# Layer 1's gate and up projections as seven block products instead of eight, in a one-core inference step

## The chip, the core and the metric

One core of a Trainium2 chip runs the kernel. The metric is the device time of one execution in microseconds, as the median of three runs. Engines are named as the profile names them: PE (TensorE), DVE (VectorE), ACT (ScalarE), POOL (GpSimd) and SP (SyncE, which issues most of the DMAs).

## What is computed

The reference is one inference step of a two-layer backbone: 512 latent tokens and 128 context tokens of width 1024 pass, in each of two layers, through four token mixers and then a gated feed-forward part. The change lies in the feed-forward part of the second layer (layer 1, counted from 0):

```python
def modulated_norm(x, g, shift, scale):
    return rms_norm(x, g) * (1 + scale) + shift

def ffn_sublayer(x, mods, p):
    h = modulated_norm(x, p['norm2_g'], mods[3], mods[4])
    y = (jax.nn.silu(h @ p['ffn_w_gate']) * (h @ p['ffn_w_up'])) @ p['ffn_w_down']
    return x + mods[5] * y
```

The widths are 1024 for the model and 2816 for the inner part. Everything is float32.

## The kernel before, in words

All 640 tokens are handled together, with features on the 128 partitions and tokens along the free dimension. A float32 matrix product is made of three matmuls in the type float32r: each operand is kept as a high part `hi` (the value cast) and a low part `lo` (the value less `hi`), and hi·hi, hi·lo and lo·hi are added in PSUM. `split` (L307) makes the two parts: the cast on ACT (L308), the subtraction on DVE (L309). `weights` (L311) brings one 128-column piece of a weight matrix (128 x 8 x 128, 512 KB) into one of three `wst` buffers by a DMA on SP and splits it into one of two `whi` and `wlo` buffers; `spare` (L325) names other tiles for the last down-projection pieces.

The feed-forward part of a layer (in `run`, from L2090) has 22 inner tiles f of 128 columns. For each, `fm_tile` (L619) makes the gate product and then the up product: 8 slices of the width times 3 matmuls times 2 token halves (256 and 384 columns), 48 matmuls each, so 96 for a tile. ACT takes silu of the gate product (L2120), DVE multiplies it with the up product out of PSUM (L2128), and the result `g` is split. The tiles run in three parts (8, 7, 7). After each part, the down projection adds the part's product to the residual `x` (L1810), in 8 output tiles e.

The first tile is special: `by_halves` (L648) makes the gate and up products of tile 0 and the gate product of tile 1 over the first 256 tokens, and during that time the norm of the other 384 tokens is finished: their sum of squares by matmul (`nst`), a reciprocal square root in eleven small DVE instructions (L377 to L383), a broadcast by matmul (`nb`), and then `norm_k` (L564) for each of the 8 slices: scaling on DVE (L571), the `hi` part on ACT (L574), and the `lo` part on DVE for even slices (L580) or, over a shifted copy made by ACT (L578), on POOL for odd ones (L584). POOL also adds the squares (L541).

PE's order of work is written out in the program. On the other engines the tile framework's scheduler sets the order; each engine then runs its queue strictly in that order, and an instruction that waits holds up what is behind it. `g`, `sg` and `h` are SBUF tiles; `acc` and `tacc` are PSUM tiles (five banks in turn for the projections).

## Time and profile before

| | |
|---|---|
| median of three runs | 1959.8 us (1953.36 to 1960.69) |
| the profiled execution | 1962.85 us, of which the span of instructions is 1961.0 us |
| PE busy / DVE / ACT / POOL over the span | 94% / 55% / 37% / 17% |
| granted PE clock, mean over the span | 0.978 |

The profile gives, for each engine, busy time, what its instructions wait for, and the chain of waits that ended last, followed back from the last instruction. A matmul row of a timeline merges neighbours of one shape: the time from one row's start to the next is what PE spent, while the duration shown includes the pipeline behind the last one. Durations of DVE and ACT instructions overlap by some hundredths of a microsecond with the next one's.

### The profile page before, as it was taken

To read this page: it belongs to the slowest core of one execution; us is meant where nothing else is said; L and a number is where in the kernel's file an instruction comes from. 1 tells how busy PE (TensorE), PEld (TensorE's weight loads), DVE (VectorE), ACT (ScalarE), POOL (GpSimd) and SP (SyncE) were. 2 spreads that over 40 slices of the span, in tenths; PEclk is the share of its full clock that TensorE was granted. 3 is DMA by queue.
4 is the path that set the end of the run, shared out by engine and by line. 5 is a ranking of instruction groups with operands and counts; after the bars stand their busy time and mean duration, and the time that the engine had idled before them with its cause. 6 is when DMAs were issued, how large, how long until landed. Compare 5 with 4: busy or idle time off the path is not lost.

```text
span 1961.0 us, 40272 instructions
## 1 busy us (share of the span) xinstructions
PE 1847.3 (94%) x16620; PEld 1742.0 (89%) x16620; DVE 1070.1 (55%) x2304; ACT 727.5 (37%) x1497; POOL 329.7 (17%) x530
## 2 busy tenths in 40 slices
PE   5998998899999999999999999789999999999997
PEld 4986787778999999999998988678889999999997
DVE  6573546677557547647555854567655232233244
ACT  4632124766442112222346322367645221221231
POOL 1221521233300000000133271123322000000001
PEclk9997899999999999999999999899999999999999
DMA  7345423142445436436423322213342222222221
GB/s 299 122 119 135 125 78 104 31 110 79 139 138 172 140 108 193 150 109 189 133 91 101 98 66 67 77 44 84 95 151 65 76 76 76 76 68 83 75 97 54
DMA packets 114166, 210.35 MB, mean 107 GB/s; under 512 B 44160, under 2 KB 61312, under 8 KB 113856
## 3 DMA queue, kind: packets, MB, share of 16 engines
q1 hardware_dynamic: 105920, 202.74, 32.8%
q0 software_dynamic: 2816, 4.72, 1.2%
q8 instruction: 130, 2.13, 0.4%
q10 hardware_dynamic: 5248, 0.33, 0.2%
q14 instruction: 52, 0.43, 0.1%
HBM read 183.14 MB, written 19.89 MB: 104 GB/s over the span
## 4 chain that ended last, share of the span: by engine, by line
PE 78%; DVE 9%; ACT 5%; DMA 5%; issue 2%; POOL 1%; SPq 0%; DVEq 0%; ACTq 0%; POOLq 0%
PE acc L351 56%; PE tacc L351 6%; PE pvo L351 2%; PE ptp L363 2%; PE sc L351 2%; PE mpart L351 1%; PE invp L351 1%; DMA wst<-wout 1%; DVE wlo L309 1%; ACT p L1294 1%; ACT whi L308 1%; DMA wmd<-wmodT 1%; DMA wmd<-wmod 1%; ACT pt L1329 1%; PE ysp L351 1%
## 5 line engine op out<-in xcount | busy, mean ns | idle before, releaser
L351 PE MATMUL acc<-h,whi 128*128 128x256 f32 (+1 forms) x3520 | 679.0, 312 | 3.2 <-ACT h L574 1.4
L351 PEld LDWEIGHTS acc<-h,whi 128*128 128x128 f32 x3520 | 578.5, 189 | 11.7 <-issue 3.4
L308 ACT CAST whi<-wst 128x1024 fp32r<-128x1024 f32 (+3 forms) x202 | 196.9, 976 | 687.9 <-PE acc L351 645.0
L351 PE MATMUL acc<-h,wlo 128*128 128x256 f32 (+1 forms) x1760 | 411.1, 310 | 0.8 <-DVE wlo L309 0.8
L309 DVE TENSOR_TENSOR wlo<-wst,whi 128x1024 fp32r<-128x1024 f32 (+3 forms) x202 | 229.9, 1139 | 204.2 <-ACT whi L308 199.3
L351 PEld LDWEIGHTS acc<-h,wlo 128*128 128x128 f32 x1760 | 320.4, 189 | 2.5 <-DVE wlo L309 1.3
L351 PE MATMUL acc<-g,whi 128*128 128x256 f32 (+1 forms) x1128 | 216.7, 309 | 0.1
L541 POOL TENSOR_TENSOR sq<-sq 128x256 f32<-128x256 f32 (+1 forms) x48 | 45.4, 947 | 927.2 <-ACT sq L535 926.9
L1810 DVE SCALAR_TENSOR_TENSOR x<-acc,mods,x 128x256 f32<-128x256 f32 (+1 forms) x192 | 75.3, 434 | 210.6 <-PE acc L351 210.4
L351 PEld LDWEIGHTS acc<-g,whi 128*128 128x128 f32 x1128 | 185.9, 188 | 0.4 <-DVE g L309 0.4
L507 DVE SCALAR_TENSOR_TENSOR wmj<-wmd,cb 128x1024 f32<-128x1024 f32 x112 | 136.8, 1222 | 40.9 <-DMA wmd<-wmodT 39.6
L351 PE MATMUL tacc<-whi,h 128*128 128x256 f32 (+1 forms) x640 | 151.2, 317 | 1.0 <-ACT whi L308 0.8
L351 PE MATMUL acc<-g,wlo 128*128 128x384 f32 (+1 forms) x564 | 135.2, 309 | 0.0
L351 PEld LDWEIGHTS tacc<-whi,h 128*128 128x128 f32 x640 | 111.4, 194 | 11.8 <-issue 6.6
L351 PE MATMUL acc<-oh,whi 128*128 128x384 f32 (+1 forms) x512 | 114.6, 314 | 3.3 <-DVE xe L1810 1.9
L363 PE MATMUL ptp<-cbase,p 128*128 128x128 f32 x512 | 80.3, 283 | 27.8 <-ACT pt L1329 14.1
L351 PEld LDWEIGHTS acc<-g,wlo 128*128 128x128 f32 x564 | 103.2, 188 | 0.0
L351 PE MATMUL tacc<-wlo,h 128*128 128x256 f32 (+1 forms) x320 | 98.2, 307 | 1.3 <-DVE wlo L309 1.3
L363 PEld LDWEIGHTS ptp<-cbase,p 128*128 128x128 f32 x512 | 56.6, 141 | 43.9 <-ACT pt L1329 17.6
L2128 DVE TENSOR_TENSOR sg<-acc,sg 128x256 f32<-128x256 f32 x88 | 39.2, 485 | 101.9 <-PE acc L351 101.9
L1297 POOL TENSOR_SCALAR dg<-cbase,sd 128x128 f32<-128x128 f32 x96 | 58.8, 613 | 207.1 <-DVE sd L1295 150.0
L1294 ACT ACTIVATE p<-sc,sm 128x768 f32<-128x768 f32 (+1 forms) x96 | 79.8, 831 | 31.8 <-DVE sm L1291 23.6
(321 smaller groups left out, 2655.9 us busy)
## 6 DMA issues: line engine op xcount, KB each, us to landing
wmd<-wmodT SPq DMA_DIRECT2D x56, 512.0 KB
wst<-wg SPq DMA_DIRECT2D x44, 512.0 KB
wst<-wu SPq DMA_DIRECT2D x44, 512.0 KB
wmd<-wmod SPq DMA_DIRECT2D x40, 512.0 KB
wst<-wd SPq DMA_DIRECT2D x34, 448.0 KB
wst<-wfm SPq DMA_DIRECT2D x24, 512.0 KB
wst<-wd SPq DMA_DIRECT2D x16, 512.0 KB
wst<-wtma SPq DMA_DIRECT2D x12, 512.0 KB
```

The lines of the kernel that those rows point to most:

```text
L308: self.nc.scalar.copy(hi, src)
L309: self.nc.vector.tensor_tensor(out=lo, in0=src, in1=hi.bitcast(F32), op=ALU.subtract)
L351: self.nc.tensor.matmul(out, lhsT, rhs, start=start, stop=stop)
L363: self.nc.tensor.transpose(out, in_, self.ident)
L507: nc.vector.scalar_tensor_tensor(out=j, in0=st, scalar=1.0, in1=self.cb[:, g], op0=ALU.mult, op1=ALU.mult, accum_out=self.msum[:, e, g:g + 1])
L541: (eng or nc.gpsimd).tensor_tensor(out=self.sq[hf][0], in0=self.sq[hf][0], in1=sq, op=ALU.add)
L1294: nc.scalar.activation(p, s, AF.Exp, bias=m, accum_out=d)
L1297: nc.gpsimd.tensor_scalar(out=dg, in0=self.ident, scalar1=d, scalar2=None, op0=ALU.mult)
L1329: nc.scalar.copy(pt[:, a:a + m].rearrange("p a b -> p (a b)"), tp[:, :128 * m])
L1810: self.nc.vector.scalar_tensor_tensor(out=x_out[:, a:b], in0=o[h][:, a - HB * h:b - HB * h], scalar=m[:, 8 * gate + e, grp:grp + 1], in1=x ...
L2128: nc.vector.tensor_tensor(out=sg[:, s], in0=ou[q], in1=sg[:, s], op=ALU.mult)
```

## The change

In layer 1, tiles 3 to 21 are made by a scheme of Strassen's kind. Stack the gate and up pieces of a tile as two block rows, cut the width into two halves of four slices and the tokens into two halves of 320 columns. The 2 x 2 block product, which takes eight block products (each 4 slices x 3 matmuls), is made from seven, of sums of blocks.

- Tokens, once: the norm of the last 384 tokens leaves its float32 result in new tiles `hraw` (`raw`, made by ACT for all slices), POOL adds `hi` and `lo` of the first 256 tokens to have their float32 values too (`raw_tokens`, four instructions of 512 columns), and during tile 0 DVE forms four sums in two steps (`sums_of_tokens`, eight instructions of 640 columns), of which three are split into the new tile `tt`. The fourth replaces half of `h` after tile 2 (`last_sum`).
- Weights, for each tile (`seven`): four sums on POOL (L771 to L774 of the changed kernel), and seven splits of 512 columns, five by ACT and DVE and two by ACT and POOL. The split operands go in turn through six pairs' worth of `whi`, `wlo` and `sw` buffers. The raw pieces have a fourth buffer (`wsx`).
- Results: one copy from PSUM on ACT and seven DVE additions from PSUM of 320 columns (L798 to L810) put the four blocks together; silu then works in SBUF, and the product with the gate is taken in SBUF (L2236).
- There are 8 instead of 12 `g` tiles in layer 1, and the last down-projection pieces find their room in `sw` and `tt` (`room`); the first two of them are split after tile 21 in the program's text, before it until now.

The core of the diff:

```diff
+    def room(self, e, l, pool, n):
+        if e == 0:
+            ts = [pool.tile([128, KD, 128], F32R, tag="sw", name="w2", bufs=2) for _ in range(2)]
+        elif e == 2:
+            t = self.left_room = pool.tile([128, 3, 2, 4, HT], F32R, tag="tt", name="w2", bufs=1)
+        if 2 <= e < 6:
...
-    def norm_k(self, l, which, hf, k, x, rb, h, pool):
+    def norm_k(self, l, which, hf, k, x, rb, h, pool, raw=None):
...
-            if k % 2:
+            if raw:
+                nc.scalar.activation(raw[:, a:b], t[:, a:b], AF.Identity, bias=bias)
+            elif k % 2:
...
             else:
...
-        if k % 2:
+        if k % 2 or raw:
             s = SPLIT[hf]
-            nc.gpsimd.tensor_tensor(out=lo[:, s], in0=t[:, s], in1=hi[:, s].bitcast(F32), op=ALU.subtract)
+            eng = nc.gpsimd if k % 2 else nc.vector
+            eng.tensor_tensor(out=lo[:, s], in0=(raw or t)[:, s], in1=hi[:, s].bitcast(F32), op=ALU.subtract)
...
+    def raw_tokens(self, h, pool):
+        self.raw = [pool.tile([128, 2, T], F32, tag="g", name="hraw", bufs=self.gbufs) for _ in range(4)]
+        for p in range(4):
+            v = [h[:, q, 2 * p:2 * p + 2, 0:HB] for q in range(2)]
+            self.nc.gpsimd.tensor_tensor(out=self.raw[p][:, :, 0:HB], in0=v[0].bitcast(F32), in1=v[1].bitcast(F32),
+                                         op=ALU.add)
+    def sums_of_tokens(self, h, pool):
...
+        tt = pool.tile([128, 3, 2, 4, HT], F32R, tag="tt", name="tt", bufs=1)
+        v = self.nc.vector.tensor_tensor
+        for p in range(2):
+            b11, b12 = self.raw[p][:, :, left], self.raw[p][:, :, right]
+            b21, b22 = self.raw[p + 2][:, :, left], self.raw[p + 2][:, :, right]
+            v(out=b11, in0=b12, in1=b11, op=ALU.subtract)
+            v(out=b12, in0=b22, in1=b12, op=ALU.subtract)
+            v(out=b22, in0=b22, in1=b11, op=ALU.subtract)
+            v(out=b21, in0=b21, in1=b22, op=ALU.subtract)
+            for i, t in enumerate((b22, b12, b21)):
+                self.split(*[tt[:, i, q, 2 * p:2 * p + 2] for q in range(2)], t)
...
+    def last_sum(self, h):
+        for p in range(2):
+            self.split(*[h[:, q, 2 * p:2 * p + 2, HT:T] for q in range(2)], self.raw[p][:, :, 0:HT])
+    def seven(self, srcs, acc, pool):
...
+        nc = self.nc
+        raw = []
+        for src in srcs:
+            self.raws += 1
+            r = (pool.tile([128, KD, 128], F32, tag="wsx", name="wst", bufs=1) if self.raws % 4 == 3 else
+                 self.wp.tile([128, KD, 128], F32, tag="wst", name="wst", bufs=3))
+            nc.sync.dma_start(out=r, in_=src)
+            raw += [r[:, 0:4], r[:, 4:8]]
+        a11, a12, a21, a22 = raw
+        def slot():
+            i = self.slots = (self.slots + 1) % 3
+            p, tag = ((self.wp, "whi"), (self.wp, "wlo"), (pool, "sw"))[i]
+            t = p.tile([128, KD, 128], F32R, tag=tag, name="sw", bufs=2)
+            return t[:, 0:4], t[:, 4:8]
...
+        g, v = nc.gpsimd.tensor_tensor, nc.vector.tensor_tensor
+        w = {}
+        w["a11"], w["s2"], w["a12"], w["s3"], w["s1"], w["a22"] = [slot() for _ in range(6)]
+        def by_pool(hi, lo, src):
+            nc.scalar.copy(hi, src)
+            g(out=lo, in0=src, in1=hi.bitcast(F32), op=ALU.subtract)
+        s2, s3, s4 = [pool.tile([128, 4, 128], F32, tag=t, name="sum", bufs=1) for t in ("s2", "s3", "s4")]
+        g(out=s3, in0=a11, in1=a21, op=ALU.subtract)
+        g(out=a21, in0=a21, in1=a22, op=ALU.add)
+        g(out=s2, in0=a21, in1=a11, op=ALU.subtract)
+        g(out=s4, in0=a12, in1=s2, op=ALU.subtract)
+        self.split(*w["a11"], a11)
+        self.split(*w["s2"], s2)
+        by_pool(*w["a12"], a12)
+        self.split(*w["s3"], s3)
+        self.split(*w["s1"], a21)
+        by_pool(*w["a22"], a22)
+        def product(a, b):
+            o = acc.tile([128, 512], F32, tag="w", name="acc")[:, 0:HT]
+            wt, tok = w[a], self.tokens[b]
+            for k in range(4):
+                for c, (i, j) in enumerate(((0, 0), (0, 1), (1, 0))):
+                    self.mm(o, wt[i][:, k], tok[j][:, k], k == 0 and c == 0, k == 3 and c == 2)
+            return o
+        sg = pool.tile([128, T], F32, tag="sg", name="sg", bufs=3)
+        up = pool.tile([128, T], F32, tag="sg", name="up", bufs=3)
+        c11, c12, c21, c22 = sg[:, 0:HT], sg[:, HT:], up[:, 0:HT], up[:, HT:]
...
+        p1 = product("a11", "b11")
+        w["s4"] = slot()
+        self.split(*w["s4"], s4)
+        p6 = product("s2", "t2")
+        nc.scalar.copy(c11, p1)
+        v(out=c12, in0=p6, in1=c11, op=ALU.add)
+        p2 = product("a12", "b21")
+        v(out=c11, in0=p2, in1=c11, op=ALU.add)
+        nc.scalar.activation(c11, c11, AF.Silu)
+        p7 = product("s3", "t3")
...
+        p5 = product("s1", "t1")
+        v(out=c22, in0=p5, in1=c21, op=ALU.add)
+        v(out=c12, in0=p5, in1=c12, op=ALU.add)
+        p4 = product("a22", "t4")
...
+        p3 = product("s4", "b22")
+        v(out=c12, in0=p3, in1=c12, op=ALU.add)
+        nc.scalar.activation(c12, c12, AF.Silu)
+        return sg, up
...
             gpool, g_st = self.pool("g", side="left")
+            by_sums = l == L - 1
+            plain = 3 if by_sums else KF
+            self.gbufs = 8 if by_sums else 12
...
                 last = lambda e, n=f1 - f0: self.weights(A["wd"][l, e, :, f0:f1], [128, n, 128],
-                                                         parts=self.spare(e, l, gpool, n))
+                                                         parts=(self.room if by_sums else self.spare)(e, l, gpool, n))
                 for f in range(f0, f1):
+                    if f >= plain:
+                        if f == plain:
+                            self.last_sum(h)
+                        sg, up = self.seven([A["wg"][l, f], A["wu"][l, f]], ps, gpool)
+                        g[f - f0] = gt = gpool.tile([128, 2, T], F32R, tag="g", name="g", bufs=self.gbufs)
+                        if f < KF - 1:
+                            nc.vector.tensor_tensor(out=up, in0=up, in1=sg, op=ALU.mult)
+                            self.split(gt[:, 0], gt[:, 1], up)
+                            continue
+                        for s in (slice(0, HT), slice(HT, T)):
+                            nc.vector.tensor_tensor(out=up[:, s], in0=up[:, s], in1=sg[:, s], op=ALU.mult)
+                            self.split(gt[:, 0, s], gt[:, 1, s], up[:, s])
...
@@ -2108,21 +2253,25 @@
                         def second():
                             rb = self.bcast(1, r[0], ps)
                             for k in range(KD):
-                                self.norm_k(l, 1, 1, k, x, rb, h, fx)
-
+                                self.norm_k(l, 1, 1, k, x, rb, h, fx, by_sums and self.raw[k // 2][:, k % 2])
+                        if by_sums:
+                            self.raw_tokens(h, gpool)
...
                         self.modulate(f, gpool)
-                    g[f - f0] = gt = gpool.tile([128, 2, T], F32R, tag="g", name="g", bufs=12)
+                    if by_sums and f == 0:
+                        self.sums_of_tokens(h, gpool)
+                    g[f - f0] = gt = gpool.tile([128, 2, T], F32R, tag="g", name="g", bufs=self.gbufs)
...
                 for e in range(2, KD):
                     done(e, e, halves[0], self.plain(steps(e, halves[0])))
-                kept.pop(2)
-                for i, e in enumerate((6, 7, 0, 1, 3, 4, 5, 2)):
+                again = 1 if by_sums else 2
+                kept.pop(again)
+                for i, e in enumerate((6, 7, 0, 3 - again, 3, 4, 5, again)):
```

The order of instructions shows the move at three places. The first is PE in the middle of the feed-forward part. Before, one product of a tile alternates between its two token halves, in rows of one matmul; `acc` is the bank, `whi` and `wlo` the split weight, `h` the tokens (the 48 rows of the product go on in this way):

```order
L351 MATMUL acc_19239<-h_16966,whi_19235 128x256
L351 MATMUL acc_19240<-h_16966,whi_19235 128x384
L351 MATMUL acc_19239<-h_16966,whi_19235 128x256
L351 MATMUL acc_19240<-h_16966,whi_19235 128x384
L351 MATMUL acc_19239<-h_16966,wlo_19236 128x256
```

Now, a whole tile (each `sw` is one pair of split operands, `tt` the token sums):

```order
L366 MATMUL acc_18069<-h_16966,sw_18042 128x320 x12
L366 MATMUL acc_18085<-tt_17685,sw_18043 128x320 x12
L366 MATMUL acc_18100<-h_16966,sw_18044 128x320 x12
L366 MATMUL acc_18115<-tt_17685,sw_18045 128x320 x12
L366 MATMUL acc_18129<-h_16966,sw_18046 128x320 x12
L366 MATMUL acc_18144<-tt_17685,sw_18047 128x320 x12
L366 MATMUL acc_18158<-h_16966,sw_18082 128x320 x12
```

In place of 96 matmuls of 256 and 384 columns in turn stand 84 of 320, in seven runs of twelve, each with a bank and an operand pair of its own.

The second place is DVE for one tile in the middle of the feed-forward part. Before (L2128 is the product with silu out of PSUM, L309 a split's subtraction, `g` the result):

```order
L2128 TENSOR_TENSOR sg_19230<-acc_19239,sg_19230 128x256
L2128 TENSOR_TENSOR sg_19230<-acc_19240,sg_19230 128x384
L309 TENSOR_TENSOR wlo_19356<-wst_19353,whi_19355 128x1024
L309 TENSOR_TENSOR g_19289<-sg_19230,g_19289 128x640
L309 TENSOR_TENSOR wlo_19417<-wst_19414,whi_19416 128x1024
```

Now (L310 is the split's subtraction, `sum` a weight sum made by POOL, L798 to L810 the additions out of PSUM):

```order
L310 TENSOR_TENSOR sw_19349<-sum_19354,sw_19349 128x512
L803 TENSOR_TENSOR up_19235<-acc_19282,sg_19234 128x320
L805 TENSOR_TENSOR up_19235<-acc_19296,up_19235 128x320
L806 TENSOR_TENSOR sg_19234<-acc_19296,sg_19234 128x320
L310 TENSOR_TENSOR sw_19351<-sum_19355,sw_19351 128x512
L808 TENSOR_TENSOR up_19235<-acc_19311,up_19235 128x320
L310 TENSOR_TENSOR sw_19352<-wst_19346,sw_19352 128x512
L810 TENSOR_TENSOR sg_19234<-acc_19325,sg_19234 128x320
L2236 TENSOR_TENSOR up_19235<-up_19235,sg_19234 128x640
L310 TENSOR_TENSOR sw_19388<-sum_19356,sw_19388 128x512
L310 TENSOR_TENSOR g_19340<-up_19235,g_19340 128x640
```

Five instructions a tile have become fourteen (the next tile's first two additions and two splits, interleaved in the same way, complete them), and the weight splits of the next tile stand between this tile's additions.

The third place is DVE in tile 0, from the last norm instruction (`nt`) to the split of the up piece of tile 1 (`wlo` out of `wst`). Before:

```order
L571 SCALAR_TENSOR_TENSOR nt_17563<-nb_17507,oms1_77,x_16970 128x128
L580 SCALAR_TENSOR_TENSOR h_16966<-nt_17556,mods1_75,h_16966 128x256
L580 SCALAR_TENSOR_TENSOR h_16966<-nt_17556,mods1_75,h_16966 128x128
L309 TENSOR_TENSOR wlo_17684<-wst_17681,whi_17683 128x1024
```

Now (two of the eight subtractions, L725, stand ahead of these rows):

```order
L726 TENSOR_TENSOR hraw_17420<-hraw_17422,hraw_17420 128x2x320
L727 TENSOR_TENSOR hraw_17422<-hraw_17422,hraw_17420 128x2x320
L602 TENSOR_TENSOR h_16966<-hraw_17423,h_16966 128x384
L728 TENSOR_TENSOR hraw_17422<-hraw_17422 128x2x320
L726 TENSOR_TENSOR hraw_17421<-hraw_17423,hraw_17421 128x2x320
L310 TENSOR_TENSOR tt_17685<-hraw_17420,tt_17685 128x640
L727 TENSOR_TENSOR hraw_17423<-hraw_17423,hraw_17421 128x2x320
L310 TENSOR_TENSOR tt_17685<-hraw_17422,tt_17685 128x640 x2
L310 TENSOR_TENSOR tt_17685<-hraw_17421,tt_17685 128x640
L728 TENSOR_TENSOR hraw_17423<-hraw_17423 128x2x320
L310 TENSOR_TENSOR wlo_17717<-wst_17714,whi_17716 128x1024
```

The weight's split now stands behind eight subtractions of token sums and four of the six splits of them.

## Rows read from the trace of the kernel before

**Rows 1.** The page: busy time and instructions of each engine; the chain's shares by engine.

```profile
PE 1847.3 (94%) x16620; PEld 1742.0 (89%) x16620; DVE 1070.1 (55%) x2304; ACT 727.5 (37%) x1497; POOL 329.7 (17%) x530
...
PE 78%; DVE 9%; ACT 5%; DMA 5%; issue 2%; POOL 1%; SPq 0%; DVEq 0%; ACTq 0%; POOLq 0%
```

**Rows 2.** Two stretches of layer 1's feed-forward part (columns in the first row).

```profile
core 0: us, PE busy (x) PEld busy (x) DVE busy (x) ACT busy (x) POOL busy (x), PEclk, DMA share, GB/s
1525.00:1595.00 70.00, 70.00 (x482) 70.00 (x481) 20.38 (x25) 17.45 (x26) 0.00 (x0) 1.00 0.25 76
1798.60:1896.60 98.00, 98.00 (x674) 98.00 (x673) 32.66 (x40) 27.80 (x39) 0.00 (x0) 1.00 0.27 91
```

**Rows 3.** SP's waits, 1500 to 1961: line <- awaited: total us, times, longest.

```profile
SPq L315 <- DVE wlo L309: 375.4, 58, 20.7
...
SPq L315 <- DMA wst<-wg: 3.1, 1, 3.1
```

**Rows 4.** DVE's timeline, two tiles in succession: start, duration, instruction, [wait <- awaited].

```profile
1553.06 0.89 DVE L2128 TENSOR_TENSOR sg<-acc,sg 128x256 f32<-128x256 f32 x2 [4.84 <-PE acc L351]
...
1567.06 0.89 DVE L2128 TENSOR_TENSOR sg<-acc,sg 128x256 f32<-128x256 f32 x2 [4.84 <-PE acc L351]
```

**Rows 5.** PE's timeline in an earlier stage with matmuls of 432 columns.

```profile
1056.38 0.56 PE L351 MATMUL tacc<-whi,h 128*128 128x432 f32 x2
...
1056.98 0.55 PE L351 MATMUL tacc<-whi,h 128*128 128x432 f32 x2
```

**Rows 6.** POOL: one line's group (shortest/mean/longest ns), two instructions of the timeline.

```profile
L966 POOL TENSOR_TENSOR decay<-cbase,fg x10: 1038/1365/2020, 94.6 to 1077.6; 128x512 f32<-128x512 f32 x10
...
1479.34 0.73 POOL L584 TENSOR_TENSOR h<-nt,h 128x256 fp32r<-128x256 f32 x1
...
1490.88 1.02 POOL L584 TENSOR_TENSOR h<-nt,h 128x384 fp32r<-128x384 f32 x1 [10.81 <-ACT nt L578]
```

**Rows 7.** DVE's groups by form: ... xcount | busy us, mean ns | idle ahead.

```profile
L309 DVE TENSOR_TENSOR g<-sg,g 128x640 fp32r<-128x640 f32 x42 | 34.4, 819 | 0.0
...
L2128 DVE TENSOR_TENSOR sg<-acc,sg 128x384 f32<-128x384 f32 x44 | 24.1, 548 | 0.0
...
L2128 DVE TENSOR_TENSOR sg<-acc,sg 128x256 f32<-128x256 f32 x44 | 18.6, 423 | 101.9 <-PE acc L351 101.9
...
L309 DVE TENSOR_TENSOR wlo<-wst,whi 128x512 fp32r<-128x512 f32 x26 | 17.8, 696 | 10.8 <-ACT whi L308 10.8
```

**Rows 8.** ACT's groups by form.

```profile
L308 ACT CAST g<-sg 128x640 fp32r<-128x640 f32 x42 | 30.7, 731 | 43.8 <-DVE sg L2128 42.6
...
L2120 ACT ACTIVATE sg<-acc 128x384 f32<-128x384 f32 x44 | 21.3, 484 | 0.0
...
L308 ACT CAST whi<-wst 128x512 fp32r<-128x512 f32 x26 | 15.8, 615 | 19.0 <-DMA wst<-wout 11.4 <-PE acc L351 6.6 <-DVE oh L348 1.1
```

**Rows 9.** Timeline: DVE and POOL at work at once, two places.

```profile
1465.54 1.00 POOL L541 TENSOR_TENSOR sq<-sq 128x384 f32<-128x384 f32 x1 [4.53 <-ACT sq L535]
...
1465.67 0.88 DVE L383 SCALAR_TENSOR_TENSOR nr<-rsa,nr 128x2 f32<-128x2 f32 x1
...
1477.28 1.23 DVE L309 TENSOR_TENSOR wlo<-wst,whi 128x1024 fp32r<-128x1024 f32 x1
...
1478.21 1.16 POOL L541 TENSOR_TENSOR sq<-sq 128x384 f32<-128x384 f32 x1 [1.88 <-ACT sq L535]
```

**Rows 10.** Timeline of tile 0: the second half's norm.

```profile
1482.10 1.22 DVE L309 TENSOR_TENSOR w<-wst,w 128x1024 fp32r<-128x1024 f32 x1
...
1485.69 0.16 DVE L383 SCALAR_TENSOR_TENSOR nr<-rsa,nr 128x3 f32<-128x3 f32 x1
...
1486.44 0.83 PE L351 MATMUL nb<-cbase,nr 128*128 128x128 f32 x6
```

**Rows 11.** Timeline: the split of tile 1's up piece, and PE behind it.

```profile
1503.16 1.23 DVE L309 TENSOR_TENSOR wlo<-wst,whi 128x1024 fp32r<-128x1024 f32 x1 [6.70 <-ACT whi L308]
...
1504.44 0.56 PE L351 MATMUL acc<-h,wlo 128*128 128x256 f32 x2 [0.41 <-DVE wlo L309]
```

More of the change, by code (lines that the diff above doesn't have):

```diff
@@ L27 @@
 SPLIT = (slice(0, HB), slice(HB, T))
+HT = T // 2
 L = 2
@@ L338, in spare @@
         return [t[:, 0:128 * n].rearrange("p (k n) -> p k n", k=n) for t in ts]
+    def room(self, e, l, pool, n):
[4 more added lines that the diff above has]
+        if 2 <= e < 6:
+            t = self.left_room.rearrange("p a b c d -> p (a b c d)")
+            ts = [t[:, 128 * n * i:128 * n * (i + 1)] for i in (2 * e - 4, 2 * e - 3)]
+        elif e:
+            return None
+        ts = [t.rearrange("p a b -> p (a b)") if len(t.shape) == 3 else t for t in ts]
+        return [t[:, 0:128 * n].rearrange("p (k n) -> p k n", k=n) for t in ts]
     def put(self, oh, k, a, src, view=None):
@@ L685, in half_steps @@
         return o
+    def raw_tokens(self, h, pool):
[5 more added lines that the diff above has]
+    def sums_of_tokens(self, h, pool):
+        left, right = slice(0, HT), slice(HT, T)
+        tt = pool.tile([128, 3, 2, 4, HT], F32R, tag="tt", name="tt", bufs=1)
[9 more added lines that the diff above has]
+                self.split(*[tt[:, i, q, 2 * p:2 * p + 2] for q in range(2)], t)
+        b = lambda q, k, s: h[:, q, 4 * k:4 * k + 4, s]
+        self.tokens = {
+            "b11": [b(q, 0, left) for q in range(2)], "t1": [b(q, 0, right) for q in range(2)],
+            "b21": [b(q, 1, left) for q in range(2)], "b22": [b(q, 1, right) for q in range(2)],
+        }
+        for i, n in enumerate(("t2", "t3", "t4")):
+            self.tokens[n] = [tt[:, i, q] for q in range(2)]
@@ L2093, in run @@
             gpool, g_st = self.pool("g", side="left")
+            by_sums = l == L - 1
+            plain = 3 if by_sums else KF
+            self.gbufs = 8 if by_sums else 12
+            self.slots = self.raws = -1
             for part, (f0, f1) in enumerate(THIRDS):
@@ L2102, in run @@
                         r = []
-                        parts = [gpool.tile([128, 2, T], F32R, tag="g", name="w2", bufs=12).rearrange("p a t -> p (a t)")
+                        parts = [gpool.tile([128, 2, T], F32R, tag="g", name="w2", bufs=self.gbufs).rearrange("p a t -> p (a t)")
                                  [:, 0:D].rearrange("p (k n) -> p k n", k=KD) for _ in range(2)]
@@ L2117, in run @@
                         og = self.fm_tile(A["wg"][l, f], lambda q, k: h[:, q, k], range(KD), ps)
-                    sg = gpool.tile([128, D], F32, tag="sg", name="sg", bufs=3)[:, :T]
+                    sg = gpool.tile([128, T if by_sums else D], F32, tag="sg", name="sg", bufs=3)[:, :T]
                     for q in range(2):
```

4 lines of the change are left out of this document (added).

## The prediction, made before the changed kernel was run

> **What bounds the kernel now.** I began with the page. PE is busy 94% of the span and holds 78% of the chain of waits, while DVE has little more than half its time filled and POOL a sixth [rows 1]. Such averages cover many stages, so I looked at the stage that changes. In two stretches of layer 1's feed-forward part PE is busy for all of the time at a granted clock of 1.00 (2.4 GHz); DVE works 29 to 33% of it, ACT 25 to 28%, POOL not at all, and the DMA share is about a quarter [rows 2]. The transfers are not near a limit: SP's waits are nearly all for buffers to be split (375.4 us over 58 waits, behind DVE), and the one transfer that is waited for itself costs 3.1 us [rows 3]. So here a shorter stream of matmuls is a shorter kernel, as long as POOL, DVE and ACT can feed it.
>
> **What a matmul costs.** The same pair of DVE instructions comes at 1553.06 and at 1567.06 [rows 4]: a tile takes 14.00 us, and with 96 matmuls, half of 256 and half of 384 columns, that is 0.1458 us for a mean of 320 columns. Whether 320 columns are priced by columns could be doubted, since no such matmul is in this trace. An earlier stage has 432: its pattern of three repeats after 0.60 us (1056.38 to 1056.98) [rows 5], so 0.200 each, 0.463 ns a column. The tiles give 0.1458/320 = 0.456 ns. Two widths agree within 2%, so I take price by columns.
>
> **The change part by part.**
>
> *PE.* A tile goes from 96 to 84 matmuls of 320 columns on the average: 84 x 0.1458 = 12.25 us, 1.75 less. Nineteen tiles (3 to 21) give **-33.25 us**. The bounds: at the rate of the 432 columns 84 x 320 x 0.463 ns = 12.45, so -29.5; 33.25 is the other end.
>
> *What must fit in 12.25 us.* POOL makes six instructions of 512 columns a tile. It has two rows of the same kind at 256 and 384 columns, 0.73 and 1.02 us; the line through them gives 1.31 at 512. The only rows of 512, on another line, go from 1.038 to 2.020 with a mean of 1.365 [rows 6]. I take 1.31, nearest in kind and close to that mean: 7.86 us a tile. DVE: five splits of 0.696, seven additions out of PSUM that lie between 0.423 (256) and 0.548 (384), so 0.486, and the product and the split of `g` at 0.819 each [rows 7]: 3.48 + 3.40 + 1.64 = 8.52. ACT: seven casts of 0.615, three instructions of 320 columns at 0.484 or less, one cast of 0.731 [rows 8]: 4.31 + 1.45 + 0.73 = 6.49. Each alone fits, POOL with 4.4 us to spare.
>
> *Chains between them.* A pair of split operands is filled again for the product six places on, so from the end of one use to the next stand five products, 5 x 1.75 = 8.75 us. Refilling takes a cast and a subtraction, 0.615 + 0.696 on DVE or + 1.31 on POOL, behind whatever else those queues hold; about 5 us are over. So I cost it at nothing; the cover is PE's five products, and were it gone, a product would start late by what the queues add. The raw weights land some 3 us after issue and are asked for a tile ahead. At the switches of the parts (after tiles 7, 14 and 21) the down projection needs the last tile's `g` only after six or seven of its slices, so I cost these at nothing as well, and the two weight pieces that are split after tile 21 instead of before at 0 to 1 us.
>
> *The port that DVE and POOL share.* POOL is new in this stage. Where the two already meet, a POOL instruction of 384 columns that starts at 1478.21 beside a DVE split that ends at 1478.51 takes 1.16 instead of 1.02 us; so 0.14 of the 0.30 us that they shared were lost and 0.16 were gained. A small DVE instruction that starts inside a POOL one takes 0.88 instead of 0.16 and ends as POOL ends [rows 9, 10]. The rows, then, show a wait for most of the other's duration. By them I count the instructions of both engines that read SBUF with two inputs as lying end to end, less 0.16 for each: POOL's six (7.86), DVE's five splits (3.48), its product and `g` split (1.64), 12.98 in all; less 13 x 0.16 = 2.08, makes 10.90, under 12.25. DVE's additions out of PSUM are not among them (one input is PSUM), and no row here has one beside POOL. If they held the port too, 3.40 more would make 14.3 us, more than the old tile; this is part of the slower rival below.
>
> The Trainium skill (SBUF — State Buffer, "Who interferes with whom") says that a DVE instruction with two SBUF inputs and a GpSimd instruction that reads SBUF exclude each other fully, for the whole instruction. By that rule the 0.16 falls away and the tile takes 12.98 us. The row with 1.16 speaks for a little less than that.
>
> *The start, tile 0.* It gets new work in two places where PE already waits on a chain. (a) POOL's four additions of 512 columns (4 x 1.31 = 5.24 us) start as soon as the first half is normed, about 1480, and meet the DVE split at 1482.10 and then the eleven small instructions that end at 1485.69 + 0.16. PE takes their result at 1486.44, so 0.59 us are spare [rows 10]. By turns of add, split, add, split, add and then the small ones between the rest, the last ends about 1488.7: 2.85 later, **+2.3** for PE. Bounds: 0, if POOL goes first and the splits slip into the gaps, and 5.24 - 0.59 = 4.6, if all four go ahead. (b) The split of tile 1's up piece, which PE waits 0.41 us for, comes on DVE after 6.70 us of idle time [rows 11]. Now eight subtractions and four splits of 640 columns stand ahead: 12 x 0.819 = 9.83; 9.83 - 6.70 = **+3.1**. Bounds: 0 (the norm's subtractions on the same queue become fewer, and idle time elsewhere takes some), and 4.8 with all six splits ahead. The norm's extra ACT instructions lie beside DVE's work in both bounds.
>
> *The sum:* -33.25 + 2.3 + 3.1 = **-27.85 us**. The profiled execution took 1962.85 us (span 1961.0), so 1935.0 for one like it. The median of the runs shown lies 3.05 below that execution, so I forecast **1932.0**. The bounds of the start alone (0 to 9.4) and of the column price (up to 3.8 less gained) give 1926.5 to 1939.8.
>
> **The rivals.**
>
> 1. *The port is held for whole durations.* The tile takes 12.98; 1.02 x 19 = 19.4 gained, 5.4 lost: -14.0, so 1945.8. For it: the small instruction that waited for all of POOL's [rows 9]. Against it: the 0.16 beside, and gaps in which only additions out of PSUM are due. It is what the page of the Trainium skill named above states. Chance 0.17.
>
> 2. *POOL becomes the bound (slower).* If POOL's 512 columns stretch beside a busy DVE, which they share the port with, the tile's period is POOL's six durations plus some 4.0 us in which DVE's and POOL's turns cannot overlap: the 5.12 of DVE's seven two-input instructions less 7 x 0.16. It equals the old 14.00, less 5.4/19 for the start, at (13.72 - 4.0)/6 = 1.62 us an instruction; above that the kernel is slower. At the slowest row of that width, 2.02 [rows 6], it is 16.1: 2.1 x 19 + 5.4 = +45, so 2005. The same place is reached if additions out of PSUM hold the port (14.3: +0.3 x 19 + 5.4 = +11, 1971). For it: the spread of those ten rows. Against: their mean, 1.365, and the rows of POOL in the norm. Chance 0.08.
>
> 3. *320 columns cost as much as 384.* From rows 4, 384 columns cost 0.175: a tile 84 x 0.175 = 14.7, +0.7 x 19 + 5.4 = +19, so 1978. Against: the 432 columns [rows 5]. Chance 0.03.
>
> 4. *In-order queues eat the gain.* Each engine has one queue, and an addition that waits for a product holds up the next tile's splits behind it. If each tile lost 1.5 us so, 0.25 x 19 - 5.4 would be left, so no change. Against: 5 us of slack for each operand. Chance 0.07.
>
> 5. *The start is hidden:* -33.25, so 1926.5. Chance 0.05.
>
> **How the numbers follow.** The forecast has the remaining 0.60. The range runs from 1924 (case 5, and some of the spread of the runs) to 1950 (case 1 with the start at its upper bound of 9.4): it leaves out cases 2 to 4, 0.18. A measurement of this kernel can tell about 0.5% from no change, 9.8 us: faster is below 1950.0, slower above 1969.6. The forecast, 1 and 5 are faster (0.82); 4 is the same (0.07); 2 and 3 are slower (0.11).
>
> **What would show it.** Right: in a stretch of tiles 8 to 20, the first addition from PSUM recurs every 12.25 us, PE is busy all the time at clock 1.00, POOL is at 60 to 65%, DVE near 70%. Rival 1 shows as a period near 13 with PE waiting for a split operand, on DVE and POOL in turn; rival 2 as POOL without idle time, instructions of 512 columns above 1.6 us, and PE waiting for line 768's results or those behind lines 773 and 774; rival 3 as PE at 100% with a period of 14.7. The start shows as two waits of PE, about 2.3 us ahead of the broadcast and 3.5 ahead of tile 1's up product. I am wrong altogether if PE's clock falls in the stretch, because waits in each tile break up its stream.

## The result and the profile after

| | before | changed |
|---|---|---|
| median of four runs | 1960.24 us | 1937.92 us (1936.36 to 1942.35) |
| the profiled execution, span | 1962.85, 1961.0 us | 1942.35, 1940.6 us |

The ratio is 0.9894, with a 95% interval of 0.9862 to 0.9926: 22.3 us less by the medians. A second set of runs gave 0.9872 (0.983 to 0.9915). The time lies in the forecast's range (1924 to 1950), 5.9 us above the forecast of 1932.0.

The page of the changed kernel, engines and chain, as in [rows 1]:

```profile
PE 1820.8 (94%) x16392; PEld 1714.9 (88%) x16392; DVE 1219.8 (63%) x2488; ACT 784.7 (40%) x1627; POOL 512.7 (26%) x648
...
PE 77%; DVE 9%; ACT 5%; DMA 5%; issue 2%; SPq 0%; POOL 0%; DVEq 0%; ACTq 0%; POOLq 0%
```

PE is 26.5 us shorter in busy time, DVE 149.7 and POOL 183.0 longer, and neither of the two holds more of the chain. By stretches (columns as in [rows 2]), five tiles of the second part and the 4.4 us behind a wait of tile 1:

```profile
1666.70:1728.20 61.50, 61.50 (x423) 61.50 (x421) 55.10 (x71) 30.40 (x55) 45.57 (x29) 1.00 0.26 79
1514.32:1518.70 4.38, 4.38 (x19) 4.38 (x20) 3.75 (x5) 1.35 (x2) 0.21 (x1) 0.61 0.63 180
```

PE has no idle time in the tiles, at a granted clock of 1.00. But DVE shows 90% and POOL 74% of the stretch. Their instructions have grown longer, as the groups by form of the changed kernel show (xcount | busy us, mean ns):

```profile
L310 DVE TENSOR_TENSOR sw<-sum,sw 128x512 fp32r<-128x512 f32 x57 | 56.8, 996 | 6.7 <-ACT sw L309 6.7
L310 DVE TENSOR_TENSOR sw<-wst,sw 128x512 fp32r<-128x512 f32 x38 | 46.5, 1223 | 8.7 <-ACT sw L309 8.2
...
L310 DVE TENSOR_TENSOR g<-up,g 128x640 fp32r<-128x640 f32 x18 | 26.8, 1488 | 2.2 <-ACT g L309 2.2
...
L805 DVE TENSOR_TENSOR up<-acc,up 128x320 f32<-128x320 f32 x19 | 9.3, 492 | 4.8 <-PE acc L366 2.9 <-DVE up L803 0.5
...
L803 DVE TENSOR_TENSOR up<-acc,sg 128x320 f32<-128x320 f32 x19 | 9.1, 480 | 3.1 <-PE acc L366 3.1
...
L768 POOL TENSOR_TENSOR sw<-wst,sw 128x512 fp32r<-128x512 f32 x38 | 57.2, 1504 | 94.0 <-ACT sw L767 52.9 <-PE acc L366 41.1
L773 POOL TENSOR_TENSOR sum<-wst 128x512 f32<-128x512 f32 x19 | 32.5, 1712 | 0.4
```

A split of 512 columns takes 0.996 to 1.223 us beside POOL and 0.696 without it, one of 640 columns 1.488 and 0.819 [rows 7]; POOL's 1.5 to 1.7 compare with some 1.3. DVE's additions with one input in PSUM take 0.48 to 0.49, which is what the 0.423 and 0.548 of [rows 7] for 256 and 384 columns give for 320. So a busy share in this profile contains the time for which an instruction waits for the other engine.

**Where the time went.** The rest of this document measures the stage, from PE's first matmul on `h` in layer 1's feed-forward part to the end. In the two executions of the changed kernel that were profiled it took 456.47 us both times; every other kernel's stage is known from one execution. What runs before it are the same instructions in all kernels here, yet they ended between 1474.84 and 1489.79 us; differences of whole times of a few us say nothing about the stage. PE's rows at the second part's ends:

```profile
1654.40 1.92 PE L366 MATMUL acc<-h,sw 128*128 128x320 f32 x12
1656.16 1.92 PE L366 MATMUL acc<-tt,sw 128*128 128x320 f32 x12
...
1740.50 0.75 PE L366 MATMUL acc<-g,whi 128*128 128x256 f32 x4
```

| piece of the stage, us | before | changed |
|---|---|---|
| first matmul on `h` to tile 3 | 45.12 | 52.29 |
| tiles 3 to 7 | 70.00 | 61.69 |
| tiles 8 to 14 | 98.00 | 86.10 |
| tiles 15 to 21 | 97.99 | 86.38 |
| two down projections, and all behind tile 21 | 170.01 | 170.01 |
| stage | 481.12 | 456.47 |

(Before, tile 3 has no mark of its own; its start is the first down projection's less five tiles of 14.00, and the matmul after three tiles of 96 starts at that time.) So the tiles gave 31.8 us, the start took 7.2 back, and the remaining pieces are the same. The start lost its time here:

```profile
1484.34 6.98 POOL L714 TENSOR_TENSOR hraw<-h 128x512 f32<-128x512 f32 x4
1485.21 1.52 DVE L310 TENSOR_TENSOR wlo<-wst,whi 128x1024 fp32r<-128x1024 f32 x1 [0.17 <-ACT whi L309]
...
1486.65 2.28 DVE L310 TENSOR_TENSOR w<-wst,w 128x1024 fp32r<-128x1024 f32 x1
...
1489.04 1.07 DVE L393 TENSOR_SCALAR nr<-rsx 128x3 int32<-128x3 int32 x1
1490.15 1.20 DVE L396 SCALAR_TENSOR_TENSOR rsa<-nr 128x3 f32<-128x3 f32 x1
1491.38 0.16 DVE L397 TENSOR_TENSOR rsa<-rsa,rsx 128x3 f32<-128x3 f32 x1
...
1492.96 0.94 PE L366 MATMUL nb<-cbase,nr 128*128 128x128 f32 x6 [2.11 <-DVE nr L398]
...
1510.48 0.85 PE L366 MATMUL acc<-h,whi 128*128 128x256 f32 x4 [0.74 <-ACT whi L309]
...
1514.32 0.56 PE L366 MATMUL acc<-h,wlo 128*128 128x256 f32 x2 [2.99 <-DVE wlo L310]
```

These are POOL's four additions of float32 tokens (6.98 us for some 5.2 us of work), the two DVE splits beside them (1.52 and 2.28, in [rows 10] 1.22), and the small instructions of the reciprocal root, of which two take over 1 us and, once POOL is through at 1491.3, the rest 0.16 each. PE waits 2.11 for their result, then 0.74 and 2.99 for tile 1's up piece, and behind the last wait runs 4.38 us at a granted clock of 0.61 (0.50, or 1.2 GHz, from 1515.29 to 1518.70).

### The profile page after: what moved, and what is told of

It reads as the page before. It is cut to its first block, busy times and chain, and to the rows that moved or that the text cites. A ratio compares the mean times of both kernels' runs of the same rounds, so it can differ in the third digit from the quotient of the medians.

```text
span 1940.6 us, 40518 instructions
## 1 busy us (share of the span) xinstructions
PE 1820.8 (94%) x16392; PEld 1714.9 (88%) x16392; DVE 1219.8 (63%) x2488; ACT 784.7 (40%) x1627; POOL 512.7 (26%) x648
## 3 DMA queue, kind: packets, MB, share of 16 engines
q8 instruction: 129, 2.11, 0.4%
## 4 chain that ended last, share of the span: by engine, by line
PE 77%; DVE 9%; ACT 5%; DMA 5%; issue 2%; SPq 0%; POOL 0%; DVEq 0%; ACTq 0%; POOLq 0%
PE acc L366 55%; PE tacc L366 6%; PE pvo L366 3%; PE ptp L378 3%; PE sc L366 2%; DMA wst<-wout 1%; PE mpart L366 1%; PE invp L366 1%; DVE wlo L310 1%; ACT p L1421 1%; ACT whi L309 1%; DMA wmd<-wmod 1%; DMA wmd<-wmodT 1%; ACT pt L1456 1%; PE ysp L366 1%
## 5 line engine op out<-in xcount | busy, mean ns | idle before, releaser
L366 PE MATMUL acc<-h,whi 128*128 128x256 f32 (+1 forms) x2304 | 453.9, 315 | 3.3 <-ACT h L589 1.4
L366 PEld LDWEIGHTS acc<-h,whi 128*128 128x128 f32 x2304 | 381.1, 191 | 11.9 <-issue 3.4
L309 ACT CAST whi<-wst 128x1024 fp32r<-128x1024 f32 (+3 forms) x164 | 156.9, 958 | 446.1 <-PE acc L366 398.1
L366 PE MATMUL acc<-h,wlo 128*128 128x256 f32 (+1 forms) x1152 | 274.1, 313 | 3.4 <-DVE wlo L310 3.4
L310 DVE TENSOR_TENSOR wlo<-wst,whi 128x1024 fp32r<-128x1024 f32 (+3 forms) x164 | 190.5, 1163 | 99.5 <-ACT whi L309 98.9
L366 PEld LDWEIGHTS acc<-h,wlo 128*128 128x128 f32 x1152 | 211.3, 190 | 5.0 <-DVE wlo L310 3.9
L366 PE MATMUL acc<-h,sw 128*128 128x320 f32 x912 | 143.6, 309 | 0.0
L366 PEld LDWEIGHTS acc<-h,sw 128*128 128x128 f32 x912 | 136.6, 188 | 0.0
L366 PE MATMUL acc<-tt,sw 128*128 128x320 f32 x684 | 109.5, 309 | 0.0
L366 PEld LDWEIGHTS acc<-tt,sw 128*128 128x128 f32 x684 | 102.6, 188 | 0.0
```

Of the source, the lines that this page charges most:

```text
L309: self.nc.scalar.copy(hi, src)
L310: self.nc.vector.tensor_tensor(out=lo, in0=src, in1=hi.bitcast(F32), op=ALU.subtract)
L366: self.nc.tensor.matmul(out, lhsT, rhs, start=start, stop=stop)
```

## The experiments

All were made as edits of the changed kernel. The changed kernel once more:

> The changed kernel once more, as the measure for the others of this batch. Theory and rival alike: a ratio to the kernel before near 0.989; in the trace the feed-forward part of layer 1, from its first matmul on h to the end, takes 456.5 us as in its first profile (1484.1 to 1940.6), the tiles 12.3 us each.

The ratio to the kernel before is 0.9872 (0.983 to 0.9915); the stage is the same to the hundredth, 456.47 us, and tile 3 begins after the same 52.29. Within the start one thing is different: the clock fell already behind the wait at `nb`, and then again behind the up piece's split (last two rows, columns as in [rows 2]).

```profile
1489.45 0.94 PE L366 MATMUL nb<-cbase,nr 128*128 128x128 f32 x6 [2.11 <-DVE nr L398]
...
1510.81 0.56 PE L366 MATMUL acc<-h,wlo 128*128 128x256 f32 x2 [2.46 <-DVE wlo L310]
...
1490.92:1494.33 3.41, 3.41 (x19) 3.41 (x18) 3.41 (x11) 3.41 (x11) 0.33 (x1) 0.50 0.01 2
1511.40:1514.81 3.41, 3.41 (x15) 3.41 (x14) 3.16 (x4) 1.08 (x2) 0.00 (x0) 0.50 0.70 203
```

PE, slower in tile 0, has no wait for ACT here and a shorter one for the split, and goes on 30.22 us after the stage's start (1480.59), as in the first execution (1514.32 less 1484.10). So the end of that split on DVE sets the time: PE's lower clock ahead of it cost nothing, and ACT's 0.74 is a part of the wait for it.

**POOL's four additions later.** `issue_after` queues an instruction behind another one of its engine; `last_lo` is POOL's subtraction for the norm's last odd slice, so each addition now follows one of those.

```diff
-        for p in range(4):
-            v = [h[:, q, 2 * p:2 * p + 2, 0:HB] for q in range(2)]
...
+    def raw_pair(self, h, p):
+        v = [h[:, q, 2 * p:2 * p + 2, 0:HB] for q in range(2)]
+        with self.tc.issue_after(self.last_lo.ins):
...
+                                if by_sums and k % 2:
+                                    self.raw_pair(h, k // 2)
```

> The four POOL additions that give the float32 tokens are queued behind POOL's own norm instructions of the second half. Theory (POOL holds the port that DVE's two-input instructions need, so the chain of the reciprocal root ends late): the wait of 2.38 us ahead of the broadcast nb goes to under 0.3 us. The sums of tokens now wait for the additions, so the wait of PE for tile 1's up piece (2.99 us) stays or grows by up to 2.5: the stage takes 454 to 456.5 us. Rival (the chain is late because DVE has other work ahead of it, not because of POOL): the wait at nb stays at 2.4.

The stage took 454.87 us. The wait at the broadcast is gone, `nb` comes 6.59 us after the stage's start, to the hundredth the value of the kernel before. The other waits grew:

```profile
1507.20 0.45 PE L366 MATMUL acc<-h,whi 128*128 128x384 f32 x1 [0.24 <-DVE h L602]
1513.66 0.44 PE L366 MATMUL acc<-h,whi 128*128 128x384 f32 x1 [3.07 <-DVE h L602]
1519.94 0.56 PE L366 MATMUL acc<-h,wlo 128*128 128x256 f32 x2 [2.25 <-DVE wlo L310]
```

The norm's own subtraction (L602) now stood on DVE behind token sums that POOL's additions beside them stretched from 0.81 to as much as 1.91 us (3.07), and the up piece's split behind the other sums (2.25). So it was POOL that delayed the reciprocal root; moving only its work hands all of the wait to the next ones: PE goes on behind the split 30.15 us after the stage's start, for 30.22 in the change. The 1.60 us that were gained come behind it, where the clock stayed at 1.00.

**The token sums later.** `last_split` is DVE's subtraction in the split of tile 1's up piece.

```diff
-                    if by_sums and f == 0:
-                        self.sums_of_tokens(h, gpool)
+                    if by_sums and f == 1:
+                        with self.tc.issue_after(self.last_split.ins):
+                            self.sums_of_tokens(h, gpool)
```

> The eight subtractions and six splits of token sums are queued on DVE behind the split of tile 1's up piece. Theory (that split was late because of the token sums ahead of it): PE's waits of 0.74 and 2.99 us in tile 0 to 1 go to under 0.6 in all, its clock does not fall behind them, the wait at nb stays at 2.4; the stage takes 451.5 to 452.5 us, some 4.5 less. Tile 3 needs the sums 20 us later, so no new wait. Rival (the norm itself is longer, since ACT makes a float32 result for all slices): a wait of 2 us or more stays there.

Stage 452.59 us. Tile 3 begins 47.39 us after the stage's start, 4.90 earlier than in the change, and all that is left over the kernel before is the wait at `nb` (45.12 + 2.27 = 47.39). The wait for the up piece is 0.42, as before the change, and the clock stays at 1.00. Tile 3 now waits 0.72 for its first split operand, and the five tiles up to 7 take 62.69, 1.00 more: the expected gain less this. With the waits of 0.74 and 2.99 gone but the one at `nb` kept, the rival (a norm that ACT's extra results make longer) fell.

**Both.**

> Both moves together. Theory: all the waits of the start are gone (2.4 at nb, 3.7 in tile 1, and the lower clock behind them): the stage takes 449 to 450 us, 7 less than the change, and the time is 6 to 7.5 us under that of the change in this batch. Rival (the waits come back in another place, at tile 3, whose sums are now ready later): less than 3 us gained, and PE waits for tt at tile 3's second product.

The expectation of the theory failed: 455.11 us, 1.4 less than the change; the ratio to the kernel before is 0.9868 (0.9833 to 0.9903). The rival had the size (less than 3 us gained), but not the place: PE waited ahead of tile 3, in the plain tile 2, 0.97 for a bank that DVE had not yet emptied (L2284) and 1.88 for the split of that tile's up piece, and its clock fell (last row, columns as in [rows 2]):

```profile
1514.05 0.74 PE L366 MATMUL acc<-h,whi 128*128 128x384 f32 x3 [0.97 <-DVE sg L2284]
...
1516.67 0.90 PE L366 MATMUL acc<-h,wlo 128*128 128x256 f32 x2 [1.88 <-DVE wlo L310]
...
1515.97:1522.80 6.83, 6.13 (x23) 6.13 (x24) 6.26 (x9) 3.07 (x7) 0.00 (x0) 0.50 0.39 104
```

Tile 3 begins 51.13 us after the stage's start, 6.0 later than in the kernel before: 2.85 of that are the two waits, and the other 3.2 go with the clock, at 0.50 from 1515.97 to 1522.80. DVE and POOL in the stretch behind the token sums:

```profile
1505.51 2.65 DVE L731 TENSOR_TENSOR hraw<-hraw 128x640 f32<-128x640 f32 x2
...
1505.95 1.53 POOL L775 TENSOR_TENSOR sum<-wst 128x512 f32<-128x512 f32 x1 [1.04 <-DMA wst<-wu]
...
1507.44 1.88 POOL L772 TENSOR_TENSOR sw<-wst,sw 128x512 fp32r<-128x512 f32 x1
...
1508.09 3.75 DVE L310 TENSOR_TENSOR tt<-hraw,tt 128x640 fp32r<-128x640 f32 x2
...
1509.28 1.87 POOL L776 TENSOR_TENSOR wst<-wst 128x512 f32<-128x512 f32 x1
...
1511.76 1.90 DVE L732 TENSOR_TENSOR hraw<-hraw 128x640 f32<-128x640 f32 x1
```

POOL has begun tile 3's weight sums, 15 us and more ahead of their use, and every token instruction of DVE that is normally 0.8 us takes up to 1.9. With the sums alone moved, the same POOL instruction met a DVE queue without a gap and was itself held:

```profile
1514.19 5.64 POOL L768 TENSOR_TENSOR sw<-wst,sw 128x512 fp32r<-128x512 f32 x1 [8.27 <-ACT sw L767]
```

That is 5.64 us for 1.3 of work, and up to 1518.7 DVE's token sums ran at full speed. Then POOL's next instructions came beside them, and three splits of the sums took 1.86 each:

```profile
1522.68 5.57 DVE L310 TENSOR_TENSOR tt<-hraw,tt 128x640 fp32r<-128x640 f32 x3
```

Which engine pays depends on which one is in first.

**Two POOL instructions more in each tile.** This and the next two load one engine in the tiles, to find what bounds them next.

```diff
-        g(out=s3, in0=a11, in1=a21, op=ALU.subtract)
+        for _ in range(3):
+            g(out=s3, in0=a11, in1=a21, op=ALU.subtract)
```

> POOL makes the sum s3 three times, so 8 instead of 6 instructions a tile. Theory (DVE's and POOL's instructions with two SBUF inputs lie end to end but for some 0.14 us each): 8 x 1.30 + 5 x 0.70 + 2 x 0.82 = 15.5, less 15 x 0.14 = 2.1, is 13.4 us a tile against 12.33: PE waits in each tile, +1.1 x 19 = +20 us or more. Rival (POOL's time alone counts): 8 x 1.30 = 10.4 us fits in 12.33, no change.

Stage 466.75 us, +10.3: between the two numbers. The single tiles tell why. I took for each tile the time from the end of the first operand's split to the start of its product. In the change it is 4.7 to 5.0 us from tile 10 to 14 and 4.6 to 4.7 from tile 17 to 21: a lead that does not shrink by more than 0.08 a tile. Here it falls from 6.9 in tile 9 to 3.9, 3.3, 1.8 and 0.6 in tile 13, and once it is spent the tiles take 13.8 us (13.79 from tile 13 to 14, 13.78 from 20 to 21). Before that PE runs at its own 12.3. With the lead spent PE waits in each tile, 0.64 for a bank that DVE's addition for p6 frees (L799) and 0.28 for a split. Tiles 18 to 20, with the lead nearly spent:

```profile
1824.01:1864.83 40.82, 38.33 (x254) 36.97 (x253) 36.40 (x42) 16.92 (x33) 38.00 (x25) 1.00 0.22 63
```

POOL is busy 93%, DVE 89%. So the theory's count by the port comes near (13.4 expected, 13.8 measured), and the rival fails: 10.4 us of POOL's own work would have fitted. A lead of some 7 us, built up again in each down projection, hid more than half of the price, which without it would be 1.46 x 19 = 27.7 us. Of the 10.3 that were paid, 1.9 lie behind tile 21, with a wait of 1.58 for a split of the down projection's weights.

**Four DVE subtractions more**, for a11, s2, s3 and s1.

```diff
+        def split2(hi, lo, src):
+            self.split(hi, lo, src)
+            v(out=lo, in0=src, in1=hi.bitcast(F32), op=ALU.subtract)
...
-        self.split(*w["s3"], s3)
+        split2(*w["s3"], s3)
```

> Four of the five DVE subtractions of the weight splits are made twice: 2.8 us a tile more for DVE, all with two SBUF inputs. Theory (port): 6 x 1.30 + 9 x 0.70 + 2 x 0.82 = 15.7, less 17 x 0.14 = 2.4, is 13.3 us a tile, +1.0 x 19 = +19 us. Rival (DVE's time alone counts): 8.4 + 2.8 = 11.2 us fits in 12.33, no change.

Stage 486.68 us, +30.2. Two tiles with the lead spent, 15.09 us each (1700.64, 1715.73 and 1730.82):

```profile
1700.64:1730.82 30.18, 26.71 (x171) 24.68 (x169) 30.11 (x37) 11.25 (x23) 18.95 (x13) 1.00 0.24 68
```

DVE is busy 30.11 of 30.18 us, although its own work is 11.3 of 15.09 a tile. The count by the port had said 13.3, so here it is 1.8 short.

**Six DVE additions from PSUM more**: the first additions of p6, p7 and p5 are made three times each.

```diff
-        v(out=c12, in0=p6, in1=c11, op=ALU.add)
+        for _ in range(3):
+            v(out=c12, in0=p6, in1=c11, op=ALU.add)
```

> Three of DVE's additions out of PSUM are made three times each (the results are not the reference's): six more of 0.48 us, 2.9 us a tile, the same time as in the experiment with four SBUF subtractions more, but with one input in PSUM. Theory (instructions with an input in PSUM do not hold the port): 11.3 us of DVE's own time, tiles stay at 12.33 to 12.5, the time within 4 us of the change. Rival (every DVE instruction keeps POOL out): 7.8 + 5.1 + 3.4 + 2.9 less overlaps is far over 12.33, +20 us or more.

The theory's number failed: stage 479.36 us, +22.9, where at most 4 were expected. Its mechanism did not: the additions kept 0.48 to 0.49 us, and POOL's instructions took no longer beside them (those of L768 took 1.50 us on the average, as in the change). What it lacked is that they stand in DVE's queue between instructions that do wait for POOL. Over three tiles:

```profile
1691.13:1733.40 42.27, 39.03 (x254) 38.51 (x253) 39.97 (x61) 17.00 (x34) 28.03 (x18) 0.96 0.23 68
```

DVE is busy 95%, and PE waits, longer than with more work on POOL, for a bank that the last of the three additions frees:

```profile
1689.26 3.79 PE L366 MATMUL acc<-h,sw 128*128 128x320 f32 x24 [0.88 <-DVE sg L799]
...
1702.99 3.79 PE L366 MATMUL acc<-h,sw 128*128 128x320 f32 x24 [1.13 <-DVE sg L799]
...
1717.70 2.69 PE L366 MATMUL acc<-h,sw 128*128 128x320 f32 x13 [2.10 <-DVE sg L799]
```

The operands still had 2 us and more to spare at that time; behind the longest of these waits the clock fell as well (0.90 from 1720 to 1733). Of the 22.9 us, 4.3 lie behind tile 21. So the tiles' next bound after PE is the length of DVE's queue with its waits for the port in it: 55.10/5 = 11.0 of 12.3 us in the change. These three runs agree on that, with DVE at 89, 100 and 95% and POOL above DVE only in the first; they don't tell how much the port alone would bear.

**Both moves, one tile earlier.**

```diff
-            plain = 3 if by_sums else KF
+            plain = 2 if by_sums else KF
```

> Both moves of the start, and the seven products from tile 2 on, so for 20 tiles. Theory: 1.67 us less than with both moves alone, if the sums of tokens are ready when tile 2 needs them: the stage takes 447.5 to 448.5 us. Rival (they are not): PE waits 1 to 5 us for tt or for the new right half of h in tile 2, and the stage takes 449 to 453 us.

Stage 459.99 us, beyond the rival's range, though by the rival's cause in the main: PE waits 5.24 us for `tt`, once, in tile 2. Two more waits lie in tile 0, in the norm of the last tokens:

```profile
1495.65 0.44 PE L366 MATMUL acc<-h,whi 128*128 128x384 f32 x1 [1.39 <-ACT h L589]
1497.11 0.44 PE L366 MATMUL acc<-h,whi 128*128 128x384 f32 x1 [1.02 <-DVE h L602]
...
1526.40 3.30 PE L366 MATMUL acc<-tt,sw 128*128 128x320 f32 x11 [5.24 <-DVE tt L310]
```

Beside both places the clock stood at 0.50 for a time (1497.99 to 1501.40 and 1525.29 to 1532.12). Tile 2 begins after 35.27 us for 31.12 in the kernel before: 2.4 by the waits, the rest by the clock. Why tile 0 waits in this run and not with both moves alone was not followed up. The ratio to the kernel before was 0.9908 (0.9892 to 0.9925).

**Two of the four additions, and the sums, later.**

```diff
+        for p in range(2):
+            self.raw_pair(h, p)
...
+                                if by_sums and k in (1, 3):
+                                    with self.tc.issue_after(self.last_lo.ins):
+                                        self.raw_pair(h, 2 + k // 2)
```

> The sums later as before, and only two of POOL's four additions behind POOL's first norm instruction of the second half; the other two start as in the change. Theory (DVE's chain has 5 us of POOL's work in its way, of which two additions still fit beside the two weight splits): the wait at nb shrinks from 2.4 to under 0.6, tile 3 begins 45.2 to 45.8 us after the stage's first matmul (the kernel before: 45.1), and the stage takes 450.3 to 451.5 us against 456.5 of the change. Rival (what DVE cannot do in tile 0 comes back in tiles 2 and 3, as with all four moved): over 453 us, with waits of PE behind line 310 in tile 2 or 3.

As the theory had it. PE's waits in the stage up to tile 3:

```profile
1486.18 0.93 PE L366 MATMUL nb<-cbase,nr 128*128 128x128 f32 x6 [0.18 <-DVE nr L398]
...
1504.26 0.56 PE L366 MATMUL acc<-h,wlo 128*128 128x256 f32 x2 [0.41 <-DVE wlo L310]
...
1525.96 1.74 PE L366 MATMUL acc<-h,sw 128*128 128x320 f32 x10 [0.72 <-DVE sw L310]
```

Tile 3 begins 45.53 us after the stage's start (before: 45.12), and the stage takes 450.22 us: 6.25 less than the change, 30.9 less than the kernel before. Of the 6.25, the start gives 6.76; tiles 3 to 7 take 1.01 back, as with the sums alone moved; and 0.50 are less behind tile 21, where the edit moves nothing (clock 0.95 there for 0.93), so 5.75 can be put down to the moves. By whole times it beats the kernel before, ratio 0.9877 (0.9854 to 0.99); against the change the whole times don't decide (median 1937.86 us), since what runs ahead of the stage varies more than 6 us.

**The products from tile 4 on**, with the four or the two additions moved.

> All four additions and the sums later, but the seven products from tile 4 on, for 18 tiles. If the waits that remained with both moves came from the first product tile needing everything too early (DVE and POOL full in tiles 1 and 2), one more plain tile takes them away: 449.2 + 1.68 = 450.9 to 451.5 us for the stage. If they come from the way the token sums lie ahead of the plain tiles' weight splits on DVE, they stay: about 455 + 1.7 = 456 to 457 us.

> As the first of this batch, from tile 4 on. If that one has no waits left, this is 1.68 us longer (452 to 453); if it has some in tile 2 or 3, this loses part of them and comes out the same or shorter.

452.79 and 453.12 us. Tile 4 begins after 58.94 us in the first, where 45.12 + 14.00 = 59.12 would be the kernel before: no wait is left in the start that the kernel before does not have, so with both moves the first product tile had indeed come too early. But behind tile 21 there are 2.0 us more (66.42 for 64.41), most of it a wait for a split of the down projection's weights:

```profile
1867.63 0.44 PE L366 MATMUL acc<-g,w 128*128 128x384 f32 x1 [1.47 <-DVE w L310]
```

The change and the runs with the moves from tile 2 or 3 on do not have it; the two with two POOL instructions or four DVE subtractions more do (1.58 and 1.57). Without these 2.0 the first would be at 450.8, near the expected 450.9. Why one tile fewer brings that wait was not followed up. The second was to be equal or shorter than the version with two additions, since that has waits left at tile 3. Up to the first down projection 1.0 of them is indeed gone (it begins after 108.90 us for 108.23, 0.67 later where one product tile less costs 1.68), but the same tail (66.14 for 63.91) makes the stage 2.9 longer.

## Why the prediction was right, and where it was off

- **PE's term** was -33.25 us, the measured one -31.8: 234.17 us for 19 tiles, 12.32 each. The step "84 x 0.1458 = 12.25" used the mean of 256 and 384 columns; 320 columns cost 0.1467 (234.17/1596 matmuls), 0.6% more. Price by columns held, PE was busy all the time at a clock of 1.00, and rival 3 (14.7 a tile) fell.
- **Start, (a):** +2.3 forecast, +2.27 measured (`nb` at 8.86 instead of 6.59 us), and by the cause given: with the additions moved it is 6.59 again. The wait was to be about 2.3 and is 2.11.
- **Start, (b):** this term was mis-sized, +3.1 for +4.90. The wait itself came near what was worked out: PE goes on behind the up piece's split 30.22 us after the stage's start for 24.60 before [rows 11], 5.62 later, and less the 2.27 of (a) that is 3.35. The sum had nothing for the clock: from there to tile 3 it is 22.07 us for 20.52, 1.55 more, with 1515.29 to 1518.70 at 0.50. With the additions alone moved the split came as late (30.15), the clock stayed at 1.00, and this way took 20.52; with the sums moved all 4.90 went.
- **The chains between engines** cost nothing, as forecast, with the spare time that was estimated: about 5 us forecast, 4.6 to 7.2 measured from the third tile of a part on, for the five operands that DVE splits. (With the sums moved, the first operand of tiles 5 to 7 has 2.0.) The switches of the parts and the end cost nothing.
- **The port.** "Less 0.16 for each" gave 10.90 us a tile. The tiles with more load give an estimate of the overlap, if the port was what bounded them: 8 x 1.30 + 5 x 0.70 + 2 x 0.82 = 15.5 took 13.8, so 0.11 for each of 15 instructions; and 15.7 took 15.09, so 0.04 for each of 17. Part of it is not work side by side: durations reach into the next instruction's, and two of 0.81 us on DVE take 1.54 in the run with the additions moved. Applied to the change, 12.98 - 13 x 0.04 to 0.11 is 11.5 to 12.5 us, and the lead shows that it is hardly more than the 12.3 that PE takes. So PE was the bound, but by this estimate by at most 0.8, not by 1.4; that the tile still fitted with the count that was too low was in part luck. How much was really spare is not shown: with the sums moved the lead of the first operand is 2.0 in tile 5 and still 2.0 in tile 7, so it does not grow back. The rule that the Trainium skill states (SBUF — State Buffer, "Who interferes with whom": the one that comes second is blocked in full) is nearer to these traces than the 0.16 that I had read from one row; by it alone the tile would have been 12.98, rival 1, and that the trace does not show: it is 12.32.
- **Rival 2** named POOL as the bound "above 1.6 us an instruction". Lines 773 and 774 took 1.7 on the average, and no PE wait followed: those durations contain the wait for DVE, so the threshold was in the wrong measure. Likewise "POOL at 60 to 65%, DVE near 70%" came out as 74% and 90%.
- **Rival 4** did not happen, but is near: six additions of 0.48 us more in DVE's queue, with no port in them, made the stage 22.9 us longer.
- The sum -33.25 + 5.4 = -27.85 became -31.8 + 7.2 = -24.65 in the stage. The profiled executions differ by only 20.5 us, because what ran ahead of the stage, the same instructions in both, took 4.2 us longer in the changed kernel's.

## What to carry to other kernels

Fewer matmuls are worth their full time where PE is the bound and the operands have a lead; look then at the stage's start, where the new operands must be made for the first time while no lead exists yet: 7.2 us of the 31.8 went there, and 5.75 came back by queueing the same instructions elsewhere. A wait there can cost more than itself: 1.55 of the 7.2 us went with the clock behind it. Where DVE and POOL both work on SBUF, count an instruction's time with its wait for the other engine, and test the margin by adding work; a lead can hide a bound for several tiles.
